# Skipped slots in the adding stores and on-chip rows for the first expert of a mixture-of-experts layer

## The chip, the cores and the metric

One NeuronCore of a Trainium2 chip runs one decoder layer. The metric is device time in microseconds of one execution, the median of several runs.

## The reference

One layer, 512 tokens of width 1024, everything in float32: RMSNorm with an adaptive scale and shift, a projection into four kinds of token mixer (differential attention, block attention, gated linear attention, a gated recurrence), an output projection with a gate, and then the part that matters here, a mixture of experts:

```python
logits = (xt @ router_w + router_b)
top_vals, top_idx = lax.top_k(logits, TOP_K)      # 4 of 32
gates = jax.nn.softmax(top_vals, axis=-1)
...
hu = xb @ w_up[e] + b_up[e]                       # 1024 -> 2048
g = jnp.minimum(hu[:, :D_FF], SWIGLU_LIMIT)
lin = jnp.clip(hu[:, D_FF:], -SWIGLU_LIMIT, SWIGLU_LIMIT)
glu = g * jax.nn.sigmoid(SWIGLU_ALPHA * g)
return ((lin + 1.0) * glu) @ w_down[e] + b_down[e]
...
x = x + g2 * moe(h)
```

Every token goes to 4 of 32 experts, so 2048 (token, expert) pairs are computed. Each expert has 12 MB of weights, 402 MB in all, and all of them are read.

## The kernel before, in words

**First part (emit_pre).** The mixers and the output projection. In this part the Tile scheduler orders each engine's instructions; generators are interleaved by `Tasks`, which always advances the generator with the least virtual time. `out_proj` (L1175) makes the layer's residual `acc[tt]` for four tiles of 128 tokens; its output weights are scaled by the gate on POOL (L1147) and split into a high and a low part on ACT (L418) and on DVE or POOL (L419). `route(tt)` (L1201) follows each tile: it stores the normalised rows to a DRAM tensor `hn` (L1220, ACT queue), computes the router's logits, the top 4, and for each token its place within each expert (`posm`, L1283). `down_bias(tt)` (L1255) adds the gated down-projection biases to `acc[tt]` (POOL, L1269) and stores that to the output (SP queue, L1271); for tiles 0 and 1 it runs in this part (OPT["db"] is 2), for tiles 2 and 3 in the next. The output has 128 spare rows behind its 512, and tile 0 is stored there too (L1273).

`first()` (L1303) gets the rows of expert 0, which is always computed first: a one-hot select per tile (L251), a small product that gives each of 128 slots its token number (L1315), an indirect gather of those rows from `hn` (POOL queue, L256), eight transposes (L264), scale and shift on ACT (L288), split on DVE (L294, L295). A slot without a token has a number past the end; the gather leaves such a row out.

**Second part (emit_moe).** PE, DVE and ACT keep the order in which the program is written. Experts are sorted by their count of tokens (`sort`, `sorted_`, L1428 to L1445). Two generators share TensorE. `whole()` (L1553) takes expert 0 and the 15 fullest ones one at a time with 128 slots, weights split into high and low parts (ACT L1503, DVE L1508) and three products for each (L1635 to L1637 up, L1654 to L1656 down); 24 steps of 0.5 MB for one expert, one unit of virtual time each. `pairs()` (L1664) takes the other 16 two at a time with 64 slots each, in plain float32 (L1700), 12 steps of 2 MB for a pair, 2 x PACE units each. The pairs wait for the flag "sorted".

Weights come by 1 MB loads on SP's queue into a ring of nine, later ten, buffers (`load`, L1483); SP waits until a buffer is free. From the second expert on the load's address comes from the sort.

`begin(k)` (L1576) spreads the start over the first eight steps of expert 0: sort and transposed `posm` at step 0, up-biases (POOL, L1467) and gates at 1, order of the experts at 2, `fill_gx` at 4, slots of expert 0 at 5, down-bias of tiles 2 and 3 at 6 and 7, the flag at 7. `slots_of` makes the one-hot selects and then at once the products that read them (L1518). Row gathers follow on POOL's queue.

At an expert's end `finish` (L1538) scales the result on DVE (L1542) and adds it to the output by an indirect DMA with addition (L1522). That add takes `rows_of(r)` slots: 128 for the first four ranks, 96 for the next twelve, 64 for each half of a pair. A slot without a token adds zeros to a spare output row.

Of the kernel before, what the change touches and what calls it, by code (L numbers as in the profile page):

```python
# [334 lines left out]
OPT = dict(pin=2, gx=10, old=1, po=1, hp=4, sp=5, am1=1, am2=0, pe=6, wt=4, m_g1=0, m_sc2=0, m_sh2=0, m_g2=1, mord=4, db=2, gw=0, rt=12.125, st=4.73)  # L335


def emit_pre(nc, tc, I, O, P, M):
# [35 lines left out]
    with tc.tile_pool(name="pre", bufs=1) as pool:  # L374
# [61 lines left out]
        with tc.tile_pool(name="pp", bufs=1, space=PSUM) as psp:  # L436
# [848 lines left out]
            def routes():  # L1285
                for tt in range(4):
# [4 lines left out]
                    if tt == 1:  # L1291
                        yield "g2"
                        yield "yfree"
                        if OPT["db"] == 0:
                            yield "out"
# [7 lines left out]
            def first():  # L1303
# [20 lines left out]
                free("xst")  # L1324
# [49 lines left out]
RAW = 10  # L1374
PACE = 1.96
NW = 15
PAIRS = (E - 1 - NW) // 2
FULL = 3


def rows_of(r):

    return 64 if r > NW else 96 if r > FULL else 128


def emit_moe(nc, tc, I, O, P, M, res):
# [6 lines left out]
    with tc.tile_pool(name="moe", bufs=1) as pool, tc.tile_pool(name="mps", bufs=1, space=PSUM, reuse_waits="tile") as psp:  # L1393
# [23 lines left out]
        raw = [M(f"raw{i}", [128, 2, 1024]) for i in range(RAW - 1)]  # L1417
        fifo = list(raw)
        xt = M("xt", [128, 8, 256])
        xgp = M("xgp", [128, 2, D])  # L1420
        G.memset(xgp, 0.0)
        pb = M("pb", [128, 4, 512])
        lb["p"], hTF = pb[:, 0:2], pb[:, 2:4].rearrange("p a (b c) -> p (a b) c", b=4)
# [59 lines left out]
        def load(r, c):  # L1483

            w = fifo.pop(0)
            fifo.append(w)
# [51 lines left out]
        def finish(y, banks, g, idx, n):  # L1538
# [4 lines left out]
            for q, ix in enumerate(idx):  # L1543
                add_rows(y[q * n:q * n + n], ix[0:n])
# [8 lines left out]
        def whole():  # L1553
# [3 lines left out]

            def slots_of(r):

                for tt in range(4):  # L1560
                    select(V, Pm, iota, posr, [(r, 0, 128)], tt)
# [14 lines left out]
            def begin(k):  # L1576

                if k == 0:
                    sort()
                    columns(posm, lb["w"][:, 1])  # L1580
                elif k == 1:
                    up_bias()
                    columns(gates, lb["p"][:, 1])
                elif k == 2:
                    sorted_()
                    by_rank(lb["w"][:, 1], posr)
                elif k == 3:
                    by_rank(lb["p"][:, 1], gatr)
                elif k == 4:
                    fill_gx()  # L1590
# [4 lines left out]
                if k == 7:  # L1595
                    M.free("bdR")
                    res["Pp"] = M("Pp", [128, 4, 128], F32R)
                    M.F.oldest = False
                    yb.append(M("yb1", [128, D]))
                    fifo.append(M(f"raw{RAW - 1}", [128, 2, 1024]))  # L1600
                    TK.done("sorted")
# [62 lines left out]
        def pairs():  # L1664
# [3 lines left out]
            Pp = res["Pp"]  # L1668

            def slots_of(i):  # L1670

                r = NW + 1 + 2 * i
                for tt in range(4):
                    select(V, Pp, iota, posr, [(r + q, q * 64, 64) for q in range(2)], tt)
# [39 lines left out]
            for i in range(PAIRS):  # L1714
# [15 lines left out]
                for hf in range(2):  # L1730
                    banks = [ps("p", 2) for _ in range(2)]
                    bias(banks, scs.pop(0), True)
                    for k in range(0, 8, 2):
# [6 lines left out]
                        if hf == 0 and k in (2, 4) and len(new) > k // 2 - 1:  # L1740
                            slots_of(new[k // 2 - 1])
# [6 lines left out]
                for f in range(0, 8, 2):  # L1748
# [6 lines left out]
                    if f == 6:  # L1755
                        finish(yb[1], banks, *sl.pop(i), 64)
# [123 lines left out]
```

## Time and profile before

| what | value |
|---|---|
| median of 3 runs | 1494.15 us (1492.62 to 1496.89) |
| the profiled execution, its own time | 1496.73 us |
| its span, first to last instruction | 1495.0 us |
| mean granted TensorE clock | 0.957 |
| busy: TensorE / VectorE / ScalarE / GpSimd | 92% / 64% / 47% / 14% |
| DMA | 479.95 MB, mean 321 GB/s |

PE is TensorE, PEld its weight loads, DVE VectorE, ACT ScalarE, POOL GpSimd, SP the queue that issues the loads. A line number such as L1269 is that of the kernel before. [...] The DMA share is the mean busy share of the core's 16 DMA engines. A row of the stretches gives busy us (and instructions) of PE, PEld, DVE, ACT and POOL in this order. A row of the timeline has start, duration, engine, line, operation, tiles, shape and count of merged instructions, then in brackets the idle time before it and what ended it. A row of the waits has the total, the number and the longest, in us. A row of a DMA queue has packets, MB and share of the 16 engines in the window.

### The profile page before, as it was taken

How to read it: one execution, taken by the hardware profiler on the slowest of the kernel's cores; microseconds unless marked ns; L12 is line 12 of the kernel's file. 1: busy time of each engine (PE TensorE's matmuls, PEld its weight loads, DVE VectorE, ACT ScalarE, POOL GpSimd, SP SyncE). 2: the span in 40 equal slices, each digit the busy share in tenths (PEclk: the TensorE clock that was granted, in tenths of full speed). 3: DMA queues.
4: the chain of work that ended last, by engine and by line, in shares of the span. 5: the costliest groups of instructions: out<-in, count | busy, mean ns of one | idle time of the engine just before them, and what ended most of it. 6: DMA issues, size and time to landing. Idle time of an engine off the chain costs nothing. (4 is left out here: it accounts for less than half of the span.)

```text
span 1495.0 us, 18867 instructions
## 1 busy us (share of the span) xinstructions
PE 1381.8 (92%) x6488; PEld 855.7 (57%) x6489; DVE 960.6 (64%) x1566; ACT 704.1 (47%) x1020; POOL 215.8 (14%) x140
## 2 busy tenths in 40 slices
PE   7998999998578999999999999999999999999995
PEld 5666465556355555565556555655655656555562
DVE  3469656656566666666666676767667666676662
ACT  5363435554335444554544355555435545444541
POOL 0005114435231002100100210010011001001001
PEclk9999999989668999999999999999999999999998
DMA  9343333434556999999999999999999999999993
GB/s 363 133 169 128 99 99 99 169 96 155 217 189 252 358 420 399 414 403 407 409 411 422 397 394 385 411 409 411 422 397 404 410 413 406 406 420 398 422 410 115
DMA packets 75243, 479.95 MB, mean 321 GB/s; under 512 B 9748, under 2 KB 10148, under 8 KB 22920
## 3 DMA queue, kind: packets, MB, share of 16 engines
q1 hardware_dynamic: 67912, 457.21, 75.8%
q0 software_dynamic: 6656, 19.41, 5.3%
q10 hardware_dynamic: 576, 2.10, 0.4%
q8 instruction: 52, 0.85, 0.2%
q14 instruction: 47, 0.39, 0.1%
HBM read 467.14 MB, written 15.73 MB: 323 GB/s over the span
## 5 line engine op out<-in xcount | busy, mean ns | idle before, releaser
L1503 ACT CAST xr<-af 128x1024 fp32r<-128x1024 f32 x228 | 238.5, 1048 | 244.8 <-PE ps_w L1637 151.5
L1508 DVE TENSOR_TENSOR ar<-af,xr 128x1024 fp32r<-128x1024 f32 x151 | 185.8, 1233 | 97.0 <-PE ps_w L1636 39.4
L1700 PE MATMUL ps_p<-af,xg 128*64 128x512 f32 x832 | 222.4, 612 | 5.0 <-DMA af<-wexp 5.0
L1635 PE MATMUL ps_w<-xr,ar 128*128 128x512 f32 x384 | 162.0, 422 | 0.0
L1637 PE MATMUL ps_w<-xr,ar 128*128 128x512 f32 x384 | 152.5, 397 | 0.0
L1522 POOL DMA_INDIRECT out<-xa,ii x16 | 33.6, 2101 | 724.1 <-DVE xa L1542 724.1
L1700 PEld LDWEIGHTS ps_p<-af,xg 128*64 128x64 f32 x832 | 66.7, 139 | 119.7 <-issue 107.7
L1636 PE MATMUL ps_w<-ar,ar 128*128 128x512 f32 x320 | 127.9, 400 | 1.1 <-DVE ar L1508 1.0
L1508 DVE TENSOR_TENSOR xr<-af,xr 128x1024 fp32r<-128x1024 f32 x77 | 94.8, 1231 | 39.8 <-issue 21.7
L1503 ACT CAST ar<-af 128x1024 fp32r<-128x1024 f32 x76 | 79.5, 1046 | 84.0 <-PE ps_w L1637 54.8
L1700 PE MATMUL ps_p<-af,af 128*64 128x512 f32 x344 | 103.1, 598 | 1.0 <-DMA af<-wexp 1.0
L1635 PEld LDWEIGHTS ps_w<-xr,ar 128*128 128x128 f32 x384 | 73.3, 191 | 40.8 <-issue 26.5
L1637 PEld LDWEIGHTS ps_w<-xr,ar 128*128 128x128 f32 x384 | 73.2, 191 | 17.7
L1508 DVE TENSOR_TENSOR ar<-af,ar 128x1024 fp32r<-128x1024 f32 x52 | 63.5, 1222 | 29.3 <-PE ps_w L1636 13.9
L1527 ACT ACTIVATE sb<-gb 128x512 f32<-128x512 f32 x48 | 30.3, 632 | 108.2 <-DVE gb L1526 108.2
L1654 PE MATMUL ps_w<-xr,ar 128*128 128x512 f32 x192 | 80.6, 420 | 0.0
L1636 PE MATMUL ps_w<-xr,ar 128*128 128x512 f32 x192 | 77.6, 404 | 1.1 <-DVE xr L1508 1.1
L1655 PE MATMUL ps_w<-ar 128*128 128x512 f32 x192 | 76.5, 399 | 0.7 <-DVE ar L1508 0.7
L1656 PE MATMUL ps_w<-xr,ar 128*128 128x512 f32 x192 | 76.5, 398 | 0.0
L1636 PEld LDWEIGHTS ps_w<-ar,ar 128*128 128x128 f32 x320 | 61.0, 191 | 14.3 <-DVE ar L1508 3.4
L418 ACT CAST ar<-xg 128x512 fp32r<-128x512 f32 (+1 forms) x70 | 40.5, 595 | 41.8 <-PE ps_acc L620 15.1
L1503 ACT CAST xr<-xa 128x1024 fp32r<-128x1024 f32 x39 | 40.8, 1046 | 39.2 <-PE ps_w L1637 25.7
(480 smaller groups left out, 2794.2 us busy)
## 6 DMA issues: line engine op xcount, KB each, us to landing
af<-wexp SPq DMA_DIRECT2D x306, 1024.0 KB, 15.0
xa<-wexp SPq DMA_DIRECT2D x39, 1024.0 KB, 14.4
xg<-wexp SPq DMA_DIRECT2D x39, 1024.0 KB, 15.5
af<-ada SPq DMA_DIRECT2D x20, 1024.0 KB, 6.4
xg<-wout SPq DMA_DIRECT2D x16, 512.0 KB, 3.5
xf<-ada SPq DMA_DIRECT2D x4, 1024.0 KB, 13.4
af<-wG SPq DMA_DIRECT2D x8, 384.0 KB, 8.2
out<-af SPq DMA_DIRECT2D x5, 512.0 KB, 3.8
```

The source lines that it names most:

```text
L418: A.copy(H, src)
L1503: A.copy(wH[i % NH], w)
L1508: V.tensor_tensor(wL[i % NL], ahead.pop(0), wH[i % NH].bitcast(F32), op=OP.subtract)
L1522: G.indirect_dma_start(out=O, out_offset=bass.IndirectOffsetOnAxis(ap=idx, axis=0), in_=y, in_offset=None, compute_op=OP.add, bounds_check ...
L1527: act(sb, gb, AF.Sigmoid, scale=1.702)
L1635: T.matmul(b, xH[:, k, cs], H[:, s], start=k == 0, stop=False)
L1636: T.matmul(b, xH[:, k, cs], L[:, s], start=False, stop=False)
L1637: T.matmul(b, xL[:, k, cs], H[:, s], start=False, stop=False)
L1654: T.matmul(b, hTH[:, f], H[:, s], start=f == 0, stop=False)
L1655: T.matmul(b, hTH[:, f], L[:, s], start=False, stop=False)
L1656: T.matmul(b, hTL[:, f], H[:, s], start=False, stop=f == 7)
L1700: T.matmul(b[q * 64:q * 64 + 64], x(c % 8 + j)[:, q * 64:q * 64 + 64], w[:, j, s], skip_group_check=True, **kw(c % 8 + j))
```

## The change

- `add_rows` allows row numbers up to S - 1 and drops the others in place of storing to spare rows; `rows_of` gives 128 for every whole expert (96 is gone), 64 for a pair's halves. The store of tile 0 to the spare rows goes, and with the new `rows_of` the limit at which an expert goes to the overflow code.
- `first()` multiplies each tile's residual with its one-hot matrix, scaled by the row's norm, into four PSUM banks; transposes, gather and slot numbers go.
- `down_bias` stores over POOL's queue. OPT["db"] is 0: tiles 0 and 1 get their down-bias in `begin` at steps 1 and 2.
- `begin` sorts at step 0, ranks at step 1, `fill_gx` at 2; the flag "sorted" comes at step 3. The buffers `xt`, `xgp`, `pb` of the pairs are made there, from the room of two load buffers (`once`) that serve the first two chunks alone.
- `slots_of` is cut in two: `select_of` writes the selects, a step or more before `slots_of` reads them.
- The turn of the first half is at step 3 instead of 2; PACE is 1.94 instead of 1.96.

```diff
-                dma(O[tt * 128:(tt + 1) * 128], acc[tt])
-                if tt == 0:
-                    dma(O[S:S + 128], acc[tt])
+                G.dma_start(O[tt * 128:(tt + 1) * 128], acc[tt])
...
-                xg = res["xgw"] = M("xgw", [128, 2, D])
-                G.memset(xg, 0.0)
-                Pm, p = res["Pm"], ps("t")
+                res["xgw"] = M("xgw", [128, 2, D])
+                G.memset(res["xgw"], 0.0)
+                Pf = M("Pf", [128, 4, 128])
+                banks = [ps("acc") for _ in range(4)]
                 for tt in range(4):
                     yield f"r{tt}"
-                    select(V, Pm, iota, posm, [(0, 0, 128)], tt)
-                    T.matmul(p[:, 0:4], Pm[:, tt], tok[:, tt], start=tt == 0, stop=tt == 3)
+                    V.tensor_scalar(Pf[:, tt], iota, posm[:, tt, 0:1], ms2[:, tt:tt + 1], op0=OP.is_equal, op1=OP.mult)
+                    for k in range(8):
+                        c = k % 2 * 256
+                        T.matmul(banks[k // 2][:, c:c + 128], acc[tt][:, k * 128:(k + 1) * 128], Pf[:, tt], start=tt == 0 and k % 2 == 0, stop=tt == 3, skip_group_check=True)
                     yield 1.0
-                _, idx = slots(V, t, tid, p)
-                gather_rows(G, HN, xg[:, 0], idx[0])
                 for k2 in range(4):
-                    p = ps("acc")
-                    gather_turn(T, p, k2, [xg[:, 0]], ident)
-                    gather_end(A, p, k2, xst[k2 % 2], cols, 128)
+                    gather_end(A, banks[k2], k2, xst[k2 % 2], cols, 128)
                     gather_split(V.tensor_copy, V, k2, xst[k2 % 2], xH, xL, 128)
...
-    return 64 if r > NW else 96 if r > FULL else 128
+    return 64 if r > NW else 128
...
-                                 compute_op=OP.add, bounds_check=S + 127, oob_is_err=True)
+                                 compute_op=OP.add, bounds_check=S - 1, oob_is_err=False)
...
                 if k == 0:
                     sort()
                     columns(posm, lb["w"][:, 1])
+                    columns(gates, lb["w"][:, 0])
+                    sorted_()
                 elif k == 1:
+                    by_rank(lb["w"][:, 1], posr)
+                    by_rank(lb["w"][:, 0], gatr)
                     up_bias()
-                    columns(gates, lb["p"][:, 1])
+                    res["down_bias"](0, lambda: ps("m", 2))
                 elif k == 2:
-                    sorted_()
-                    by_rank(lb["w"][:, 1], posr)
+                    fill_gx()
+                    res["down_bias"](1, lambda: ps("m", 2))
                 elif k == 3:
-                    by_rank(lb["p"][:, 1], gatr)
+                    M.free(*(f"once{i}" for i in range(len(once))))
+                    M.F.oldest = False
+                    for n in ("xt", "xgp", "pb"):
+                        res[n] = M(n, [128, 4, 512])
+                    G.memset(res["xgp"], 0.0)
+                    res["Pp"] = M("Pp", [128, 4, 128], F32R)
+                    TK.done("sorted")
                 elif k == 4:
-                    fill_gx()
+                    select_of(0)
...
-                        if hf == (r == 0) and k in ((0, 1) if r == 0 else (3, 5)) and len(new) > k // 4 + (r == 0 and k):
-                            slots_of(new[k // 4 + (r == 0 and k)])
-                        if hf and k == 2:
+                        for i, n in enumerate(new):
+                            at_ = (8 * hf + k) - (7 if r == 0 else 1) - 2 * i + (i if r == 0 else 0)
+                            if at_ == 0 and n > 1:
+                                select_of(n)
+                            elif at_ == 2 - (r == 0):
+                                slots_of(n)
+                        if hf and k == 3:
                             turn(0)
...
                     for n in new:
+                        select_of(n)
+                        yield 0.5
                         slots_of(n)
                         yield 0.5
-                    yield 2.0
+                    yield 1.5
```

## Rows read from the trace of the kernel before

**Rows 1.** Stretches: length, busy us by engine, granted clock, DMA share, GB/s

```profile
383.00:396.00 13.00, 6.76 (x44) 5.95 (x43) 8.18 (x36) 8.41 (x16) 0.38 (x1) 0.72 0.69 243
...
396.00:411.60 15.60, 2.94 (x16) 2.35 (x15) 5.78 (x23) 3.01 (x8) 1.21 (x1) 0.50 0.52 202
...
411.60:470.00 58.40, 45.56 (x182) 32.50 (x184) 39.13 (x100) 22.06 (x31) 16.84 (x10) 0.70 0.56 210
...
500.00:1470.00 970.00, 940.58 (x4110) 564.24 (x4106) 645.38 (x858) 470.35 (x557) 84.81 (x48) 0.99 1.01 405
```

**Rows 2.** Timeline from the last one-hot select to the first expert product

```profile
395.93 0.29 DVE L251 TENSOR_SCALAR ar<-cst,posm 128x128 fp32r<-128x128 f32 x1
...
402.09 1.21 POOL L256 DMA_INDIRECT xg<-hn,ii  x1 [18.71 <-DMA hn<-af]
...
407.26 1.97 PE L264 MATMUL ps_acc<-cst,xg 128*128 128x128 f32 x8 [9.71 <-DMA xg<-hn,ii]
...
407.98 1.51 ACT L288 ACTIVATE af<-ps_acc,col_sh,col_sc 128x128 f32<-128x128 f32 x4 [12.33 <-PE ps_acc L264]
...
410.06 1.51 ACT L288 ACTIVATE af<-ps_acc,col_sh,col_sc 128x128 f32<-128x128 f32 x4 [0.57 <-DVE ar L295]
...
411.62 0.79 PE L1635 MATMUL ps_w<-ar,ar 128*128 128x512 f32 x1 [2.40 <-ACT af L288]
```

**Rows 3.** Waits of PE from 405 to 500 us

```profile
PE ps_m L1518 <- DVE ar L251: 9.9, 5, 3.0
```

**Rows 4.** Waits of PE from 500 us to the end

```profile
PE ps_m L1535 <- DVE xa L1530: 6.6, 5, 2.0
...
PE ps_m L1518 <- DVE ar L251: 6.3, 8, 2.5
...
PE ps_p L1700 <- DMA af<-wexp: 6.0, 5, 2.3
```

**Rows 5.** fp32 products of L1450, at half and full clock

```profile
414.48 1.86 PE L1450 MATMUL ps_m<-cst,posm 128*32 128x128 f32 x8
...
417.86 1.06 PE L1450 MATMUL ps_m<-cst,gates 128*32 128x128 f32 x8
```

**Rows 6.** Timeline of POOL at the end of the output projection

```profile
368.90 1.27 POOL L419 TENSOR_TENSOR ar<-xg,ar 128x512 fp32r<-128x512 f32 x1 [0.73 <-ACT ar L418]
...
372.40 1.27 POOL L1269 TENSOR_TENSOR af<-af,af 128x512 f32<-128x512 f32 x1 [2.23 <-DVE af L1268]
...
373.63 2.36 POOL L1147 TENSOR_TENSOR xg<-xg,af 128x1024 f32<-128x1024 f32 x1
```

**Rows 7.** Timeline of PE, one down-bias in the expert stage

```profile
433.47 0.65 PE L1260 MATMUL ps_m<-cst,gates 128*32 128x128 f32 x6
...
435.82 0.63 PE L1635 MATMUL ps_w<-xr,ar 128*128 128x512 f32 x1
```

**Rows 8.** Waits of SP's queue from 370 to 500 us

```profile
SPq L1271 <- POOL af L1269: 30.6, 4, 12.5
```

**Rows 9.** POOL DMA queue: 645-651, 405.2-406.9, 406.2-406.85 us, whole span

```profile
q0 software_dynamic: 144, 0.52, 43.8%
...
q0 software_dynamic: 144, 0.21, 33.5%
...
q0 software_dynamic: 22, 0.07, 26.4%
...
q0 software_dynamic: 6656, 19.41, 5.3%
```

**Rows 10.** Timeline of the end: two products of a whole step, two adds

```profile
1473.92 0.40 PE L1654 MATMUL ps_w<-xr,ar 128*128 128x512 f32 x1
...
1474.16 0.40 PE L1655 MATMUL ps_w<-ar 128*128 128x512 f32 x1
...
1481.93 1.41 POOL L1522 DMA_INDIRECT out<-af,ii  x1 [4.65 <-issue]
...
1486.93 1.40 POOL L1522 DMA_INDIRECT out<-af,ii  x1 [3.59 <-DMA out<-af,ii]
```

More of the change, by code (lines that the diff above doesn't have):

```diff
@@ L334 @@
 SPEED = dict(gd=0.587, gc=2.041, projs=0.642, cd=0.596, a=0.724, b=0.157, mod0=7.028, mod2=0.281, out=0.162, route=1.95, first=1.4)
[L335 removed]
+OPT = dict(pin=2, gx=10, old=1, po=1, hp=4, sp=5, am1=1, am2=0, pe=6, wt=4, m_g1=0, m_sc2=0, m_sh2=0, m_g2=1, mord=4, db=0, gw=0, rt=12.125, st=4.73)
 def emit_pre(nc, tc, I, O, P, M):
@@ L1293, in routes @@
                         yield "yfree"
-                        if OPT["db"] == 0:
-                            yield "out"
                         load_bdn()
@@ L1308, in first @@
                 xst = [xst_[:, i].rearrange("p (a b) -> p a b", a=2) for i in range(2)]
-                xg = res["xgw"] = M("xgw", [128, 2, D])
-                G.memset(xg, 0.0)
-                Pm, p = res["Pm"], ps("t")
+                res["xgw"] = M("xgw", [128, 2, D])
+                G.memset(res["xgw"], 0.0)
+                Pf = M("Pf", [128, 4, 128])
+                banks = [ps("acc") for _ in range(4)]
                 for tt in range(4):
                     yield f"r{tt}"
-                    select(V, Pm, iota, posm, [(0, 0, 128)], tt)
-                    T.matmul(p[:, 0:4], Pm[:, tt], tok[:, tt], start=tt == 0, stop=tt == 3)
+                    V.tensor_scalar(Pf[:, tt], iota, posm[:, tt, 0:1], ms2[:, tt:tt + 1], op0=OP.is_equal, op1=OP.mult)
+                    for k in range(8):
+                        c = k % 2 * 256
+                        T.matmul(banks[k // 2][:, c:c + 128], acc[tt][:, k * 128:(k + 1) * 128], Pf[:, tt], start=tt == 0 and k % 2 == 0, stop=tt == 3, skip_group_check=True)
                     yield 1.0
-                _, idx = slots(V, t, tid, p)
-                gather_rows(G, HN, xg[:, 0], idx[0])
                 for k2 in range(4):
-                    p = ps("acc")
-                    gather_turn(T, p, k2, [xg[:, 0]], ident)
-                    gather_end(A, p, k2, xst[k2 % 2], cols, 128)
+                    gather_end(A, banks[k2], k2, xst[k2 % 2], cols, 128)
                     gather_split(V.tensor_copy, V, k2, xst[k2 % 2], xH, xL, 128)
-                free("xst")
+                free("xst", "Pf")
             SP = SPEED
@@ L1374 @@
 RAW = 10
-PACE = 1.96
+PACE = 1.94
 NW = 15
 PAIRS = (E - 1 - NW) // 2
-FULL = 3
 def rows_of(r):
-    return 64 if r > NW else 96 if r > FULL else 128
+    return 64 if r > NW else 128
 def emit_moe(nc, tc, I, O, P, M, res):
@@ L1416, in emit_moe @@
         lb = {"w": yl[:, 2:4]}
[L1417 to L1423, printed above, removed]
+        once = [M(f"once{i}", [128, 2, 1024]) for i in range(2)]
+        raw = [M(f"raw{i}", [128, 2, 1024]) for i in range(RAW - 2)]
+        fifo = once + raw
         gb, sb = t("gb", [128, 512]), t("sb", [128, 512])
@@ L1485, in load @@
             w = fifo.pop(0)
-            fifo.append(w)
+            if r or c >= len(once):
+                fifo.append(w)
             if r == 0:
@@ L1543, in finish @@
             for q, ix in enumerate(idx):
-                add_rows(y[q * n:q * n + n], ix[0:n])
+                o = q * (128 // len(idx))
+                add_rows(y[o:o + n], ix[0:n])
         def bias(banks, sc, first):
@@ L1556, in whole, with select_of, slots_of @@
             at = lambda r: (r + 1) % 2 * 128 if r else 0
-            def slots_of(r):
+            def select_of(r):
                 for tt in range(4):
                     select(V, Pm, iota, posr, [(r, 0, 128)], tt)
+            def slots_of(r):
                 sl[r] = slot_mm(Pm, lambda tt: gx[:, tt, r])
@@ L1596, in begin @@
                     M.free("bdR")
-                    res["Pp"] = M("Pp", [128, 4, 128], F32R)
-                    M.F.oldest = False
+                    select_of(1)
                     yb.append(M("yb1", [128, D]))
-                    fifo.append(M(f"raw{RAW - 1}", [128, 2, 1024]))
-                    TK.done("sorted")
+                    for i in (RAW - 2, RAW - 1):
+                        fifo.insert(0, M(f"raw{i}", [128, 2, 1024]))
             later = []
@@ L1668, in pairs, with select_of @@
             Pp = res["Pp"]
-            def slots_of(i):
+            xt = res["xt"].rearrange("p a (b c) -> p (a b) c", b=2)
+            xgp = res["xgp"].rearrange("p (a b) c -> p a (b c)", a=2)
+            lb["p"], hTF = res["pb"][:, 0:2], res["pb"][:, 2:4].rearrange("p a (b c) -> p (a b) c", b=4)
+            def select_of(i):
                 r = NW + 1 + 2 * i
@@ L1674, in slots_of @@
                     select(V, Pp, iota, posr, [(r + q, q * 64, 64) for q in range(2)], tt)
+            def slots_of(i):
+                r = NW + 1 + 2 * i
                 sl[i] = slot_mm(Pp, lambda tt: gx[:, tt, r:r + 2].rearrange("p r c -> p (r c)"), 2)
@@ L1739, in pairs @@
                             bias_of(i, 1)
-                        if hf == 0 and k in (2, 4) and len(new) > k // 2 - 1:
-                            slots_of(new[k // 2 - 1])
+                        for n in new if hf == 0 else ():
+                            if k == 2 * (n - i) - 2:
+                                select_of(n)
+                            elif k == 2 * (n - i):
+                                slots_of(n)
                         if hf and new:
@@ L1755, in pairs @@
                     if f == 6:
-                        finish(yb[1], banks, *sl.pop(i), 64)
+                        finish(yb[1], banks, *sl.pop(i), rows_of(r0))
                     yield 2 * PACE
```

## The prediction

> **What bounds the kernel now.** I first cut the span into stretches by what runs in them and read busy time, granted clock and DMA share of each [rows 1]. [...]
>
> Second view, the timeline at the seam [rows 2]. The last one-hot select of the router is at 395.93; then come the product with the token numbers, an indirect gather of rows that the ACT queue has only just stored, eight transposes at 407.26, ACT and DVE for scale and split, and the first expert product at 411.62. TensorE waits 9.7 us for the gather alone. That is a pure chain of 15.7 us.
>
> Third view, the waits. In the start of the stage TensorE waits 9.9 us for one-hot selects (L251) that are issued right ahead of the products that read them [rows 3]. In the body it waits 6.6 us for L1530 and 6.3 us for L251, and only 6.0 us for weights [rows 4]. So where TensorE stops in the body it is mostly for DVE, while the DMA engines have no free time.
>
> About 0.3% (4.5 us) is what a measurement of this kernel tells from no change.
>
> **The change, part by part.**
>
> *A. First expert's rows on chip.* Removed: four small products, the slot arithmetic, the gather, eight transposes. Added: per token tile one DVE instruction (as L251, 0.29 us) and eight fp32 products of 128x128x128. A product is two records: eight records of this kind took 1.86 us at half clock and 1.06 at full [rows 5], so a tile's sixteen cost 3.7 or 2.1 us. After the last select: 0.3 (select) + 0.4 (hand-over, an estimate from the gaps of [rows 2]) + 0.9 (a quarter of 3.7, until the first bank is whole) + 3.6 (first ACT at 407.98 to first expert product at 411.62, kept as it is) = 5.2; I write 5.5. Gain 10.2 us. The other three tiles' 24 products cost 6.4 us at full clock and 11.2 at half; they are ready earlier and use banks that are free once the output projection is out, but TensorE is idle only 6.2 of the 13 us before 396 [rows 1]. If none fits there, the gain becomes a loss of 1 us; if all fit it is 10.2. Nearer to fitting, as the idle time is about their price: I charge 2 us. **A = -8 us** (-10.2 to +1).
>
> *B. Down-bias of the first two tiles leaves the projection.* On POOL, in order, the bias add L1269 waited 2.2 us for DVE and ran at 372.40, and the scaling L1147 of the last output weights stood behind it until 373.63; POOL had ended its previous work at 370.17 [rows 6]. Without the add L1147 may start there: 3.4 us sooner, and both last tiles hang on it. Lower end nothing (its other inputs might be late). **B = -3 us.**
>
> *C. Sooner sort, new order at the start.* Selects are issued a step or more ahead of their products: the 9.9 us [rows 3] go. Two more down-biases come in: 433.47 to 435.82 for one, 2.35 us [rows 7]: +4.7. Their stores, and those that held SP's queue for 30.6 us of waits on POOL [rows 8], go to POOL's queue; the loads behind them on SP get free, worth nothing by itself as TensorE had no wait for weights here, but without it the earlier pairs would starve. New waits: the pairs start after step 3 instead of 7, their gathers stand on POOL behind the up-bias split, four bias adds, two stores and the memset, and the transposes that need them are in TensorE's order with the first expert's products behind them. By the one gather shown, issue 402.09 to 407.26, one takes 5.2 us [rows 2]; two whole steps and a down-bias cover some 5 us of it: I charge +3 (0 to +8). [...] **C = -5 us** (-13 to +6). Selection of slots, memset and the freed buffers are on DVE, POOL and SP beside this.
>
> *D. The body: adding stores skip unused slots.* Added rows before: 4 of 128, 12 of 96 and 16 of 64, that is 2688; used slots are 512 x 4 = 2048. A 128-row add with nothing else in its queue took 43.8% of 16 engines for 6 us [rows 9], 0.33 us of an engine per row. So 640 rows are worth 640 x 0.33 / 16 = 13 us of all engines, if the engines share them evenly. They don't have to: in the last 0.65 us of the first gather (0.21 MB, so 51 used of 128 slots) the queue kept only 26.4% of the engines busy [rows 9], so a slot belongs to an engine, and the used slots come first. Before, a 96-row add gave each engine 6 rows; now a 128-slot add gives the engines of the low slots 8 and those of the high slots few or none. On the low engines twelve adds grow by 2 rows: 24 x 0.33 = 7.9 us more, not less. Every weight load needs all sixteen. Against that, TensorE loses 6.6 + 6.3 us of waits [rows 4]: the turn is one step later and the selects two sooner. Ends: -13 (TensorE decided, its waits vanish, DMA has room) and +12 (the low engines decide and no slack takes up their 7.9; I add half as much for bunching, an estimate). The DMA share of 1.01 is the nearest row, so I don't take the gain; but the waits that go let TensorE catch up between adds. **D = +3 us.**
>
> *E. The tail.* Before, the last pair step is ordered behind the last whole step, and three adds run one after another behind the products: 1481.93 to 1486.93 is 5.0 us for one [rows 10]. With the pairs starting 3.5 steps sooner and the new pace (95 x 3.88 = 369 instead of 372), their last step has six whole steps behind it, 6 x 6 x 0.24 = 8.6 us [rows 10], and both their adds overlap these. Left is one add after the products; its low engines have 8 rows instead of 6 (0.7 us). **E = -4 us** (-5 to +1).
>
> Priced at nothing: the removed spare-row store, the two memsets, one buffer instead of another for the first two weight chunks; all on POOL or SP in stretches with idle DMA.
>
> **Sum.** -8 -3 -5 +3 -4 = -17. The profiled execution took 1496.73, 2.6 above the median of the runs, 1494.15. 1496.73 - 17 = 1479.7; against the median 1477. I predict 1477.
>
> **The rivals.** *Products late* (0.16): the Tile scheduler puts all 32 products behind the last router tile, at the half clock that [rows 1] show there. A falls to nothing: 1485. For it: the four small products that they replace also ran together at the end. Against: those shared one bank with the router, these don't.
>
> *Even relief* (0.12): the skipped rows give 13 us to all loads and TensorE's waits go as well; D is -13: 1461. For it: the DMA share of 1.01. Against: the gather's 26.4%.
>
> *Crowded low engines* (0.06), the slower side: the engines of the low slots set the body. D is +12, and a lead of TensorE from A to C then shows only as waits for weights, as it must not outrun the loads; the tail keeps -4: 1494 + 8 = 1502. [...]
>
> *No effect* (0.04): the start's gain waits for the weights and D takes the tail's: 1494.
>
> **How the numbers follow.** The forecast has 0.62; its own range is 1469 to 1485. Low end of the range: even relief and most of C, 1462. High end: late products, the pair gathers at +8 and half of D's upper end, 1490. Faster: 0.62 + 0.12 + 0.14 of late products = 0.88; same 0.06; slower 0.06.
>
> **What would show it.** Right: the last select to the first expert product is 5 to 9 us; no wait of TensorE for L251; first pair product 20 us or more sooner than before; fewer bytes in POOL's DMA queue (19.41 MB before [rows 9], less 691 rows of 4 KB: 16.6); the pairs' adds before the last whole product; the body from 30 us after the start no shorter than before, with waits for weights in place of those for DVE. Wrong: TensorE stands at the pairs' first transposes for over 10 us; the body shrinks by 10 us (even relief) or grows by 10 (crowded engines); the weights' landing times lengthen while the mean DMA share falls.

## The result and the profile after: slower by 0.6%, lost in the start and in the body

The changed kernel takes 1505.82 us (median of 5 runs, 1502.16 to 1508.82), the kernel before beside it 1496.09 (5 runs): ratio 1.0057, 95% interval [1.0044, 1.0071]. The prediction said 1477 and faster. The profiled execution took 1502.5 us (span 1500.7, mean granted clock 0.97, as a share of TensorE's full speed), 5.8 more than that of before.

I took the difference apart by equal work: each expert product counts with its time at full clock (a whole step 1.4 us, a pair step 3.65, 888 us in all), and the table below puts the times at which a kernel has done so much of it against those of the kernel before.

```
work done, us        0.5    10    20    50   350   650   887
changed kernel     -13.5  +2.1  -4.9  +5.4  -0.9  +1.8 +10.6
```

TensorE begins the experts 13.5 us sooner and is 5.4 us late by 50 us of work; the body, from there to the last product, adds 10.6 - 5.4 = 5.2; behind the last product 4.8 come back (16.6 us to the end of the span before, 11.8 after): 5.4 + 5.2 - 4.8 = 5.8. The pairs' steps stand elsewhere among the whole steps than before, so points within the body swing (level at 120 us of work, 10 late at 500); two kernels with the same order compare more firmly.

The stretches of the changed kernel, cut and laid out as [rows 1]:

```profile
383.00:396.00 13.00, 10.57 (x87) 10.11 (x86) 9.75 (x44) 7.84 (x17) 0.00 (x0) 0.86 0.56 189
396.00:411.60 15.60, 13.32 (x67) 10.08 (x67) 8.14 (x23) 6.51 (x12) 5.17 (x3) 0.72 0.11 45
411.60:470.00 58.40, 38.43 (x148) 23.29 (x146) 39.19 (x92) 18.14 (x25) 22.85 (x17) 0.81 0.59 230
500.00:1470.00 970.00, 932.62 (x4080) 557.06 (x4076) 635.97 (x849) 467.46 (x552) 82.62 (x48) 0.99 1.00 403
```

From 396 to 411.6 us TensorE now works 13.3 us in place of 2.9, and the DMA share falls from 0.52 to 0.11. From 411.6 to 470 it works 38.4 us where it worked 45.6: the stretch with little work has moved, not gone. Few loads are issued in it: SP's queue reads each expert's number into a register (L1482), some 0.56 us each, and in the changed kernel all 31 of these, and one other register load, stand in a row from 404.2 to 426.9 us. Between 393.6 and 432.4 us one weight load is issued; the kernel before issues six there and has two of its register loads before 430 us.

The seam, which answers to [rows 2]: the changed kernel's timeline, the last select on DVE (L1311), the on-chip products (L1314), the first expert product (L1638).

```profile
393.02 0.34 DVE L1311 TENSOR_SCALAR af<-cst,posm,ms 128x128 f32<-128x128 f32 x1
...
389.62 0.91 PE L1314 MATMUL ps_acc<-af,af 128*128 128x128 f32 x6
393.41 3.78 PE L1314 MATMUL ps_acc<-af,af 128*128 128x128 f32 x16 [0.54 <-DVE af L1311]
398.14 0.79 PE L1638 MATMUL ps_w<-ar,ar 128*128 128x512 f32 x1 [0.95 <-ACT af L288]
```

The last select is 2.9 us sooner, and 5.1 us lie between it and the first expert product, where 15.7 lay before. The products of the other three tiles end at 390.5, in idle time.

Next, the cost of the first 50 us of work. First the kernel before, from its first expert product until so much is done, in the columns of [rows 1]:

```profile
411.62:503.20 91.58, 78.76 (x331) 51.57 (x332) 58.66 (x123) 40.92 (x56) 16.84 (x10) 0.81 0.65 247
```

The same stretch of work in the changed kernel:

```profile
398.14:508.60 110.46, 83.78 (x352) 51.85 (x352) 67.17 (x131) 42.21 (x59) 28.01 (x19) 0.86 0.57 222
```

The same work takes 18.9 us more: 5.0 more of busy time and 13.9 more of idle time. TensorE does not spend more time at half clock than before: a granted clock of 0.86 over 110.46 us makes some 31 us at half, 0.81 over 91.58 some 35. But part of them now falls on the first pair's products. Three of these in the changed kernel's timeline, two at half clock and one at full:

```profile
456.66 1.12 PE L1713 MATMUL ps_p<-xg,af 128*64 128x512 f32 x1 [0.93 <-DMA xg<-wexp]
...
475.51 1.12 PE L1713 MATMUL ps_p<-xg,af 128*64 128x512 f32 x1
...
478.30 0.59 PE L1713 MATMUL ps_p<-xg,af 128*64 128x512 f32 x1
```

The clock is at half from 450.3 to 460.5 and from 474.2 to 477.6 us; before, it was back at full by 460.5, ahead of the first pair product at 469.3. The first two pair steps, each from its first product to the end of its last, take 13.1 us in place of 7.3; 0.9 of the difference is the wait in the first row, the rest is about the 5.0 us of busy time.

The waits of PE in the stretch of the changed kernel (total, number, longest):

```profile
PE ps_m L1267 <- DVE gTd L1262: 6.2, 4, 3.4
PE ps_m L264 <- DMA xg<-hn,ii: 5.7, 1, 5.7
PE ps_m L1509 <- DVE ar L251: 4.7, 2, 2.7
PE ps_p L1713 <- DMA af<-wexp: 3.4, 1, 3.4
PE ps_m L264 <- ACT af L288: 3.0, 1, 3.0
PE ps_m L264 <- DMA af<-hn,ii: 1.1, 1, 1.1
...
PE ps_p L1713 <- DMA xg<-wexp: 0.9, 1, 0.9
```

Before, the selects cost 9.9 us there [rows 3], the down-bias 1.4, gathered rows 0.3 and weights nothing. The selects went down to 4.7; the down-bias (L1267), gathered rows (L264) and the pair's first weights (L1713) came in with 4.8, 6.5 and 4.3 more than before. The longest single wait in the changed kernel's timeline, POOL's gather and PE around it:

```profile
463.65 0.50 PE L1509 MATMUL ps_m<-gx,ar 128*128 128x4 f32 x4
...
465.13 1.77 POOL L256 DMA_INDIRECT xg<-hn,ii  x1 [13.50 <-DVE ii L278]
...
474.68 0.90 PE L264 MATMUL ps_m<-cst,xg 128*128 128x128 f32 x3 [5.68 <-DMA xg<-hn,ii]
```

The rows of the third expert are asked for at step 9 of the first and wanted at step 12: 9.5 us from the gather's issue to the transposes, with three steps of 1.4 us to cover them.

In the body the adds do move less. All DMA packets, the queue of the loads (q1) and POOL's queue (q0), each with packets, MB and share of the 16 engines, from 500 to 1455 us in the kernel before:

```profile
DMA packets 56748, 388.85 MB, mean 407 GB/s; under 512 B 7299, under 2 KB 7299, under 8 KB 11333
...
q1 hardware_dynamic: 51021, 371.55, 93.7%
q0 software_dynamic: 5664, 16.53, 7.0%
```

The same in the changed kernel:

```profile
DMA packets 56858, 384.85 MB, mean 403 GB/s; under 512 B 8171, under 2 KB 8171, under 8 KB 11659
...
q1 hardware_dynamic: 50782, 369.80, 93.6%
q0 software_dynamic: 6016, 14.30, 5.9%
```

POOL's queue takes 1.1% less of all engines, 10.5 us of the 955, and yet the loads' queue moves 1.8 MB less too (the other 2.2 of the 4.0 MB are the adds' own). A DMA record does not name its engine, so I count packets: in this stretch at least sixteen are in flight 98.1% of the time before and 94.3% after. A weight load reports sixteen completions; from the first to the last of them it takes 4.7 us in the mean before and 7.3 after (loads from 500 us on). The waits of PE from 500 us to the end, which answer to [rows 4]:

```profile
PE ps_p L1713 <- DMA af<-wexp: 7.9, 6, 3.0
PE ps_m L1526 <- DVE xa L1521: 6.6, 3, 2.6
PE ps_m L264 <- DMA xg<-hn,ii: 6.2, 3, 3.4
PE ps_p L1713 <- DMA xg<-wexp: 5.2, 4, 2.4
```

Waits for DMA are 19.3 us in place of 7.1. The 6.3 for selects are gone, the 6.6 for the turn (the transposes of an expert's activations) are not.

### The profile page after: what moved, and what is told of

It is laid out like the page before. It is cut to its first block, busy times and chain, and to the rows that moved or that the text cites. A ratio compares the mean times of both kernels' runs of the same rounds, so it can differ in the third digit from the quotient of the medians.

```text
span 1500.7 us, 18946 instructions
## 1 busy us (share of the span) xinstructions
PE 1381.6 (92%) x6540; PEld 854.3 (57%) x6541; DVE 964.1 (64%) x1562; ACT 705.5 (47%) x1020; POOL 217.2 (14%) x143
## 3 DMA queue, kind: packets, MB, share of 16 engines
q0 software_dynamic: 7472, 18.68, 4.7%
## 5 line engine op out<-in xcount | busy, mean ns | idle before, releaser
L1494 ACT CAST xr<-af 128x1024 fp32r<-128x1024 f32 x189 | 197.9, 1048 | 214.0 <-PE ps_w L1640 112.2
L1713 PE MATMUL ps_p<-af,af 128*64 128x512 f32 x632 | 228.0, 614 | 9.9 <-DMA af<-wexp 9.9
L1499 DVE TENSOR_TENSOR ar<-af,xr 128x1024 fp32r<-128x1024 f32 x126 | 154.4, 1228 | 70.1 <-PE ps_w L1639 33.8
L1638 PE MATMUL ps_w<-xr,ar 128*128 128x512 f32 x384 | 161.2, 420 | 0.0
L1494 ACT CAST xr<-xg 128x1024 fp32r<-128x1024 f32 x98 | 102.6, 1048 | 99.4 <-PE ps_w L1640 40.5
L1713 PE MATMUL ps_p<-xg,af 128*64 128x512 f32 x288 | 119.0, 616 | 5.0 <-DMA xg<-wexp 4.9
L1713 PEld LDWEIGHTS ps_p<-af,af 128*64 128x64 f32 x632 | 63.5, 140 | 91.2 <-issue 78.4
L1499 DVE TENSOR_TENSOR ar<-xg,xr 128x1024 fp32r<-128x1024 f32 x65 | 79.3, 1222 | 52.6 <-PE ps_w L1639 24.4
L1713 PE MATMUL ps_p<-af,xa 128*64 128x512 f32 x352 | 102.8, 599 | 0.0
L1638 PEld LDWEIGHTS ps_w<-xr,ar 128*128 128x128 f32 x384 | 73.3, 191 | 44.2 <-issue 26.0
L1499 DVE TENSOR_TENSOR xr<-af,xr 128x1024 fp32r<-128x1024 f32 x63 | 77.6, 1232 | 30.0 <-issue 18.2
L1513 POOL DMA_INDIRECT out<-af,ii x16 | 29.9, 1868 | 326.0 <-DVE af L1533 259.6
## 6 DMA issues: line engine op xcount, KB each, us to landing
af<-wexp SPq DMA_DIRECT2D x268, 1024.0 KB, 15.5
```

The costliest lines, as they stand in the source:

```text
L1494: A.copy(wH[i % NH], w)
L1499: V.tensor_tensor(wL[i % NL], ahead.pop(0), wH[i % NH].bitcast(F32), op=OP.subtract)
L1638: T.matmul(b, xH[:, k, cs], H[:, s], start=k == 0, stop=False)
L1713: T.matmul(b[q * 64:q * 64 + 64], x(c % 8 + j)[:, q * 64:q * 64 + 64], w[:, j, s], skip_group_check=True, **kw(c % 8 + j))
```

## The experiments

Ratios are to the kernel before, run beside each. Lag (+) or lead (-) is at equal work, as above.

**Adds as before.** The changed kernel with the old adds: 96 slots for twelve experts, unused slots to spare rows, tile 0 stored there again.

```diff
-    return 64 if r > NW else 128
+    return 64 if r > NW else 96 if r > 3 else 128
...
-  compute_op=OP.add, bounds_check=S - 1, oob_is_err=False)
+  compute_op=OP.add, bounds_check=S + 127, oob_is_err=True)
```

> The changed kernel with the adding stores as they were (96 slots for ranks 4 to 15, zeros added to spare output rows, which tile 0 is stored to again). Theory, crowded low engines: in the changed kernel the skipped slots lie on the engines of the high slots, and the used ones crowd the others; the body (equal work, from some 500 to 1470 us) grew by 8 us for that, so undoing it gives them back: 1498 (1495 to 1501). Rival, even relief: the skip saved 13 us of all engines and something else cost more, so undoing it costs: 1518. Third: the adds are hidden either way and the body grew for another reason: 1506.

1497.95 us, 1.0010 [0.9994, 1.0025]. Lag +5.9 at 50, +4.9 at 887: the body's loss is gone, the start's is whole. At least sixteen packets are in flight 97.9% of the body and a load's completions come within 4.7 us. The order of work is that of the changed kernel, which lags 0.5 us less at 50 and 5.7 more at 887. New start and new tail cancel; what leaves the change slower than the kernel before is the skipping adds.

**Skipping adds alone,** in the kernel before.

```diff
-    return 64 if r > NW else 96 if r > FULL else 128
+    return 64 if r > NW else 128
...
-  compute_op=OP.add, bounds_check=S + 127, oob_is_err=True)
+  compute_op=OP.add, bounds_check=S - 1, oob_is_err=False)
```

> The kernel before with the skipping adds alone (128 slots for every whole expert, rows past 511 dropped, no spare rows). Theory, crowded low engines: 8 us slower than the kernel before, 1504 (1500 to 1508), with the spread between the first and the last engine's share of a weight load wider than before. Rival, even relief: 13 us faster, 1483. Third, hidden adds: 1496.

1501.61 us, 1.0029 [1.0014, 1.0044]. -1.1 at 50, +4.8 at 887: the body loses 5.9 with the old start too, half of the 12 of *Crowded low engines*; the time is in the expected range, though under its 1504. At least sixteen packets are in flight 94.5% of the time, and a load's completions come within 6.6 us.

**Spread slots.** The changed kernel; only the numbering of slots differs. Slot 64h + 4a + b gets rank 32b + 2a + h (pairs: slot 4a + b rank 16b + a), so that the ranks in use, which are the low ones, lie all over the 128 slots.

```diff
+ V.tensor_copy(iotaW.rearrange("p (h a b) -> p h a b", h=2, a=16),
+               iota.rearrange("p (b a h) -> p h a b", b=4, a=16))
+ V.tensor_copy(iotaP.rearrange("p (a b) -> p a b", a=16), iota[:, 0:64].rearrange("p (b a) -> p a b", b=4))
...
-  select(V, Pm, iota, posr, [(r, 0, 128)], tt)
+  select(V, Pm, iotaW, posr, [(r, 0, 128)], tt)
```

> The changed kernel with the slots renumbered: consecutive places within an expert go to slots of different DMA engines (the one-hot selects compare with a permuted row of numbers, two small copies make it). The same rows are gathered and added. Theory, crowded low engines: the 8 us that the body grew go, and as the skip now relieves all engines up to 13 us more come, less whatever TensorE then limits: 1490 (1484 to 1498). Rival, the engine of a slot does not matter: 1506.

1483.3 us, 0.9899 [0.9880, 0.9917], 22 us less than the changed kernel and just under the expected range. The start is no better (+8.2 at 50), the body gains 16.5 (-8.3 at 887). Its DMA from 500 to 1455 us, the same view as above:

```profile
DMA packets 57951, 392.80 MB, mean 411 GB/s; under 512 B 8294, under 2 KB 8294, under 8 KB 11782
...
q1 hardware_dynamic: 51871, 377.72, 95.0%
q0 software_dynamic: 6016, 14.30, 5.9%
```

The same 6016 packets and 14.30 MB in POOL's queue, but 377.72 MB of loads in place of 369.80; at least sixteen packets are in flight 98.3% of the time, a load's completions come within 5.0 us, and the waits for DMA from 515 us on fall from 19.3 to 7.5:

```profile
PE ps_m L264 <- DMA xg<-hn,ii: 3.3, 2, 1.9
PE ps_p L1717 <- DMA xg<-wexp: 3.0, 3, 2.0
PE ps_p L1717 <- DMA af<-wexp: 1.2, 1, 1.2
```

**Spread slots with the old start:** the kernel before, skipping adds and the spread numbering.

> The kernel before with two edits alone: skipped slots in the adds (as the run that had only this, 1501.6 us) and the spread numbering of the slots. Start, order of selects and tail stay as before. Theory (the low engines cost the skipping adds what they gain, and the new start of the changed kernel is worth nothing): the spread takes off what it took off the changed kernel, 1505.8 - 1483.3 = 22, so about 1480; the other way, from the run with spread and new start: 1483.3 - 8.2 (lag of that run behind the kernel before at equal work, 50 of 888 us in) + 4.8 (old tail) = 1480. Range 1476 to 1486, DMA share of the body 1.01 with all engines busy together again. Rival (the spread pays only together with selects issued sooner, since a faster queue leaves TensorE waiting for DVE): 1488 to 1496, with the waits for the selects and the turn grown by 5 us or more.

1484.34 us, 0.9913 [0.9884, 0.9942]. Lag 0.0 at 50, -12.1 at 887, close to the even relief that I had worked out as 13 us. At least sixteen packets are in flight 97.4% of the time, which is less than in the kernel before. The waits for the selects stay (6.0 us in the body) without growing; the rival fell. So start, order and tail of the changed kernel were together worth nothing. The numbering also spreads the rows that are gathered, and these skipped slots before the change too; no run spreads the adds alone, so how much of the gain is the gathers' stays open.

**New buffers last.** In the changed kernel SP stood 15.7 us at a load into a buffer whose old content POOL was still storing (L1271). Those two buffers go to the end of the ring:

```diff
-                        fifo.insert(0, M(f"raw{i}", [128, 2, 1024]))
+                        fifo.append(M(f"raw{i}", [128, 2, 1024]))
```

> The changed kernel with the two late load buffers put at the end of the ring instead of its front, one word changed. Theory: the pairs' first weights went into room that the last down-bias stores free at 448.6 us, so SP's queue stood from 432.8 to 448.8 and TensorE waited 5.3 us at the first pair products and started the body with an empty pipeline; with free buffers the loads start some 20 us sooner and the lead of 13 us at the first expert product is kept in part: 1498 (1492 to 1502). Rival: the body is bound by the DMA engines from then on and the lead is lost anyway: 1506.

1504.95 us, 1.0045 [1.0028, 1.0062]: no gain, outside the expected range and near the rival's 1506. The loads came sooner and no pair waited for weights, but TensorE then stood at the pair's gathered rows (1.1 became 3.6 us) and still 5.3 us at the second gather; +6.7 at 50.

**Pairs later:** spread slots, the flag "sorted" at step 7.

```diff
-                    TK.done("sorted")
...
                         fifo.insert(0, M(f"raw{i}", [128, 2, 1024]))
+                    TK.done("sorted")
```

> The changed kernel with spread slots, the flag for the pairs raised at step 7 in place of step 3; all else of its start stays. Theory (new waits of the start decide, of which the pairs' are two: 3.5 us for the first weights and 2 to 5 us for gathered rows): these go, the down-bias waits stay; the pairs end some 3 steps later and the tail grows by up to 4.8: 1483 (1479 to 1488), first pair product 15 us later. Rival (the sooner start of the pairs is itself what loses the lead, as TensorE takes pair work while nothing is loaded): 1472 to 1478.

1482.02 us, 0.9905 [0.9874, 0.9936]. -3.5 at 50, 11.7 us better than with the early flag, but -16.5 at 887, only 8.2 better, and the later pairs lengthen the tail: the time is within the theory's range. So the early pairs brought in much of the start's loss, and the flag's place alone does not decide the time. With the late flag only 5 of the 32 register loads stand before 430 us, so the pairs' start is not all that moved.

**Start mended:** spread slots and three edits.

```diff
-                    fill_gx()
                     res["down_bias"](1, lambda: ps("m", 2))
+                    fill_gx()
...
                     slots_of(0)
+                    select_of(1)
                 else:
+                    slots_of(k - 5)
+                    if k == 6:
+                        select_of(2)
...
-                        fifo.insert(0, M(f"raw{i}", [128, 2, 1024]))
+                        fifo.append(M(f"raw{i}", [128, 2, 1024]))
```

> The changed kernel with spread slots, and three edits to its start: the second down-bias goes ahead of the filling of gx on DVE, the two late load buffers go to the end of the ring, and the slots of the second and third expert are found two steps sooner (steps 6 and 7). Theory (the lead of 13.5 us is lost to TensorE's new waits in the start, and a lead that survives the start passes through the body, because loads follow what TensorE has used up): the waits for gathered rows at the second gather (5.0 us), for the pair's first weights (3.5) and one down-bias (2.7) go, some 3 us come back as waits for the pairs' own rows; 1483.3 - 8 = 1475 (1470 to 1479). Rival (the body is set by the DMA engines alone and takes any lead back): 1483, within 3 us, with the lag at equal work of 50 us gone from +8 to 0 and given back later as waits for weights.

1467.86 us, 0.9806 [0.9776, 0.9836]: 15.4 us less than with the spread alone, and under the expected range. -8.3 at 50 and -24.9 at 887, so the body's own gain (16.6) is that of the spread kernel (16.5) and the whole lead reaches the end. The stretch of the first 50 us of work in this kernel:

```profile
398.20:494.90 96.70, 79.57 (x351) 52.76 (x351) 65.19 (x131) 41.88 (x59) 27.47 (x19) 0.84 0.67 261
```

PE's waits in that stretch:

```profile
PE ps_m L1513 <- DVE ar L251: 8.6, 2, 7.5
PE ps_m L1271 <- DVE gTd L1266: 3.9, 3, 1.9
PE ps_w L1645 <- ACT af L288: 2.3, 1, 2.3
PE ps_m L264 <- DMA af<-hn,ii: 2.0, 1, 2.0
```

96.7 us in place of the changed kernel's 110.5: no second gather, no weights among the waits, and the DMA share of the stretch rises from 0.57 to 0.67. The first two pair steps are back at 7.3 us. Of the register loads 20 in place of 32 stand before 430 us, and two weight loads go out at 405 and 406 us.

**Parts of the mending,** on the spread kernel: slots sooner alone, then order and ring alone.

> The spread kernel with one of the three edits to the start alone: slots of the second and third expert at steps 6 and 7. Theory (the rows gathered too late for step 12 are the largest of the new waits): the 5.0 us there go, and nothing else; the pair's weights still come late (3.5 us) and the down-bias wait stays: 1483.3 - 5 = 1478 (1475 to 1481). Rival (this wait is the whole: work issued behind it is what costs): 1468 to 1472, as with all three edits.

> The spread kernel with the other two edits alone: the second down-bias ahead of the filling of gx, and the two late load buffers at the end of the ring. Theory (edits add up: 15.4 in all, 5 of it from the slots): 1483.3 - 10 = 1473 (1470 to 1478). Rival (as the ring alone changed nothing on the changed kernel, these two are worth no more than the 2.7 us of the down-bias wait): 1480 to 1483.

Slots sooner: 1478.11 us, 0.9882 [0.9864, 0.9900], 5.2 us less, as the theory had it; the wait for the pair's weights grew to 7.4. Order and ring: 1479.45 us, 0.9906 [0.9874, 0.9937], 3.9 less, by its median nearer to the rival's 1480 to 1483 than to 1473 (its six runs spread from 1477.9 to 1490.1); the second gather kept its 5.2. Together the edits are worth 15.4, apart 9.1. By these waits, each alone leaves one that the other takes away, and work then stands at that one.

**Mended, not spread:** the three edits on the changed kernel.

> The changed kernel with the three edits to its start and without the spread slots. Theory (start and body are two separate losses that add up): the mended start took 1483.3 - 1467.9 = 15.4 us off the spread kernel and takes as much off the changed kernel: 1505.8 - 15.4 = 1490 (1486 to 1495), the spread of the engines in a weight load stays near 7 us and all sixteen are busy together some 94% of the body. Rival (in the body that the low engines set, TensorE's lead shows only as waits for weights, as these engines can't be ahead): 1500 to 1506, lead at equal work -8 at 50 of 888 and near 0 at 600.

1492.44 us, 0.9968 [0.9956, 0.9980], 13.4 less than the changed kernel. -7.0 at 50 and -1.1 at 887: the body still loses its 5.9, and the lead passes through it. Start and body are separate losses; the rival, in which the body keeps the lead, fell.

**On-chip rows alone:** the kernel before with `first()` of the changed one and db 0; the two down-biases stand at steps 1 and 4, and seven load buffers serve until step 7, then ten.

```diff
-  m_g2=1, mord=4, db=2
+  m_g2=1, mord=4, db=0
...
                     columns(gates, lb["p"][:, 1])
+                    res["down_bias"](0, lambda: ps("m", 2))
...
                     fill_gx()
+                    res["down_bias"](1, lambda: ps("m", 2))
```

> The kernel before with the on-chip rows of the first expert and what they need: no down-bias in the first part (tiles 0 and 1 get theirs at steps 1 and 4 of the first expert) and seven load buffers in place of nine until step 7, then ten as before. Sort, selects, pairs, adds and tail stay as before. Theory (a lead of the start passes through the body, less what the start puts in its place): 13.5 us of lead, less two down-biases at 2.35 and two waits for them of 1 to 3 us each: 5 us left, 1497 - 5 = 1492 (1488 to 1495), lag or lead at equal work the same at 50 and at 880 of 888 us within 2. Rival (the two down-biases hide in holes that are there anyway): 1484. Other rival (the shorter ring starves the start or the body takes the lead back): 1497 or more.

1493.85 us, 0.9972 [0.9952, 0.9992]. The lead is 13.8 us at the first product, 6.6 at 20 us of work, and between 6.6 and 7.5 from there to 887, as the theory had it. The half that is lost goes in the first 20 us of work; of the waits mainly those for the down-bias (1.4 to 5.9 us) grew there. PE's waits of this kernel from 396 to 503 us:

```profile
PE ps_m L1515 <- DVE ar L251: 10.2, 5, 3.0
PE ps_m L1267 <- DVE gTd L1262: 5.9, 4, 3.6
```

**Filling first:** the mended kernel with `fill_gx` at step 1 and both early down-biases at step 2.

> The spread kernel with the mended start (1467.9 us) and one more change of order: gx is filled at step 1, right after the ranks, and both early down-biases stand at step 2. Theory (the longest wait that is left in its start, 7.5 us for the first pair's selects, which stand behind the filling of gx and the second down-bias on DVE, shrinks to 3 or 4): 1464 (1461 to 1467). Rival (the filling then stands ahead of the low halves of the weights and TensorE waits there instead): 1467 to 1471.

1469.04 us, 0.9795 [0.9765, 0.9825], no different from 1467.86 and above the expected range. Its waits from 398 to 496 us:

```profile
PE ps_m L1271 <- DVE gTd L1266: 8.4, 4, 4.9
PE ps_m L1513 <- DVE ar L251: 3.8, 2, 2.7
```

The selects' wait shrank from 8.6 to 3.8 and the down-bias took it over, 3.9 to 8.4. The rival's sum held, but the wait moved to the down-bias, not to the low halves of the weights.

## Why the prediction was wrong, step by step

The parts of the sum measured -13.5 (A and B), +18.9 (C), +5.2 (D) and -4.8 (E), together +5.8 in place of -17.

**A and B held.** I had -8 and -3; the first expert product came 13.5 us sooner, 2.9 of it from the last select (B said 3) and 10.6 from select to product (A's best end was 10.2). The 2 us charged for the other tiles' products were not needed. *Products late* fell.

**C failed, by 24 us:** -5 forecast, and the first 50 us of work took 18.9 us more. This is the step that made the prediction wrong. Its terms were priced one by one, three of them from the wrong rows. "Selects are issued a step or more ahead of their products", and so 9.9 us were to go: 4.7 stayed. The two down-biases were priced at TensorE's 2.35 us [rows 7]; the chain PE, ACT, DVE, PE in each was not priced, and in the changed kernel the filling of gx stands ahead of it on DVE: 4.8 us of new waits. The pairs' gathers were charged with 3 us by the single gather's 5.2, and I never placed the gathers of the second and third expert, which the new order asks for three steps ahead of their use: 5.7 us. And "the earlier pairs would starve", which I had named, did happen for 4.3 us. With these taken away by three small edits 15.4 us came back on the spread kernel and 13.4 on the changed one. That is shown. C's sum also holds -3 for less time at half clock, the author's estimate, which no run shows by itself: in the first 50 us of work the time at a granted clock of 0.50 went from some 35 us to 31, but around these waits it fell on the first two pair steps, which took 5.8 us longer; C had no term for that. Nor had it one for the register loads that the sooner sort puts in a row on SP's queue; no run moves these alone, so their share of the 18.9 us is open.

**D: right mechanism, wrong value.** I took +3 between -13 and +12; the body lost 5.2, and 5.9 with the skipping adds alone. "The waits that go let TensorE catch up between adds" did not decide. The run with the old adds and the runs with the spread numbering show that the adds' bytes are not what costs: with the same bytes, spread slots turn +5.2 into -8.3 - 8.2 = -16.5. The low engines' 12 us in the rival were too much by about half. The even relief's -13 came near the measured -12.1, but that is in part luck, as the 13 counted the adds' rows alone and the numbering spread the gathered rows too. That slots in use at the low end keep only some of the engines busy shows where POOL's queue has the engines to itself, at the end: the last add of the changed kernel, with rows in 65 of its 128 slots (0.27 MB), kept 47.9% of the sixteen engines busy from 1493.8 to 1496.4 us, the last 64-slot add of the kernel before, with a row in each, all of them (107.9% by the same view) from 1488.9 to 1490.5. The body agrees as far as it can without a record naming an engine: with only the places of the used slots changed, the time with at least sixteen packets in flight went from 94.3 to 98.3%, and of a load's sixteen completions the ninth comes 0.9 us behind the eighth in the mean in the changed kernel and 1.5 with the skipping adds alone, but 0.2 before and with spread slots, as if eight of the sixteen were held up.

Where the loads reach TensorE is the pair steps, 2 MB each. One takes 3.65 us from its first product to the end of its last if its weights are there; the 94 behind the first two take, in us:

```
kernel before              365.5     changed kernel                375.3
skipping adds alone        368.7     changed, adds as before       366.6
spread slots, old start    352.7     spread slots                  359.3
                                     start mended, not spread      373.2
                                     start mended                  355.0
```

The spread takes 16 to 18 us off these steps each time. The lists of waits show only a part of that. The products of a pair's two halves run at the same time (at 1096.44 and 1096.45 us of the kernel before one of each starts, 0.59 us long), and where one half's weights are late the other's run alone and count as busy: the step that begins at 1093.89 has two products of one half alone in its first 1.07 us and took 2.1 us more than 3.65, and the list has 1.0 of that as a wait. From the kernel before to spread slots with the old start these steps fall by 12.8 us and the waits for DMA by 4.7 (7.1 to 2.4). And the kernel before and the one with the skipping adds alone stay within 1.4 us of each other for the first 500 us of work, so the full DMA share did not mean that the loads set the pace throughout.

**E held:** -4 forecast, -4.8 measured.

**The signs.** From the last select to the first expert product it took 5.1 us, and both adds of the last pair came before the last whole product, as forecast. But TensorE still waited 4.7 us for selects in the start, the first pair product came 15.5 us sooner and not 20, and POOL's queue moved 18.68 MB and not 16.6, as the four down-bias stores had moved there.

**The rivals.** *Crowded low engines* gave 1502, and the profiled run took 1502.5, but partly by chance: it put +12 in the body and let the loads take back all of the lead. The body lost half of that, and a lead is not taken back: it stays at 6.6 to 7.5 us from 20 to 887 us of work in the run with on-chip rows alone. The start's lead was lost in the start. Why a lead passes through a body whose DMA is full: SP's loads wait for buffers that come free behind TensorE's work, so work done sooner starts loads sooner. From 500 us on in the kernel before SP waited 631.0 us for DVE's split of weights (L1508) and 37.6 for the pairs' products (L1700), and the splits on DVE and ACT (L1503) in their turn 128.7 and 346.4 us for whole experts' products. That explanation fits those runs; I tried nothing that would separate it from others.

**Left open:** why the median of the on-chip run gained 3.7 us where its profiled run is 6.9 faster than that of before (their spreads, 1489.85 to 1495.14 and 1492.41 to 1502.25, overlap), and which waits would be left after the down-bias and the selects at the start of the mended kernel.

## What to carry to other kernels

In this kernel adds that skip slots saved time only when the used slots lay spread over all 128. Where ranks are dense from the low end, number the slots so that neighbours in rank are far apart; here this takes two copies of a constant and gave 17 us with the old start (1501.6 to 1484.3) and 22 with the new one. A chain that is cut at the head of a stage pays only if every later consumer in TensorE's order is placed again: for each gather, select and copy, count the steps between its issue and its use against its own measured latency. Skipping adds, on-chip rows, spread slots and the mended start together took 1467.9 us, 0.9806 of the kernel before.

## What the runs showed of the hardware that was not expected

Fewer bytes in one queue went with fewer in the other: with 14.30 MB in place of 16.53 in the adding queue, the loads' queue moved 369.80 MB in 955 us in place of 371.55, and with the same 14.30 MB in other slots 377.72. The full DMA share of the profile (1.00 and 1.01) did not tell the three apart. The time with at least sixteen packets in flight showed the crowding (94.3% against 98.1 and 98.3%), but it does not rank kernels by time: it is 97.4% with spread slots and the old start, 12 us faster than the kernel before.
